# Attention products over all rows and in pairs of heads, and one 512-column product for both operand parts in the 256-token FFNs

## Chip, cores and metric

The kernel runs on one core of a Trainium2 chip. The metric is the device time of one execution in microseconds (us). The engines are named as the profile names them: PE is TensorE's matrix products and PEld its weight loads, DVE is VectorE, ACT is ScalarE, POOL is GpSimd, SP issues the large DMAs.

## What is computed

Two transformer blocks follow each other on 256 tokens of width 1024. The first has two layers with a context of 256 further tokens: a gated linear attention (512 tokens in all) with its FFN, then a latent attention (MLA, 8 heads) whose queries are the 256 main tokens alone, with its FFN. The second block has three mixers side by side, which are 8 heads of dilated attention, a depthwise convolution and 4 heads of attention to a memory of 256 tokens, and then its FFN.

```python
x = x + g1[:, None, :] * o
x = x + g2[:, None, :] * conv_ffn(modulate(x, norm_ffn[i], sh2, sc2), ...)
...
sm = jnp.einsum("bshd,bmhd->bhsm", qm, km).astype(jnp.float32) * (HEAD_DIM ** -0.5)
pm = jax.nn.softmax(sm, axis=-1)
mo = jnp.einsum("bhsm,bmhd->bshd", pm, vm.astype(jnp.float32))
...
f = rms_norm(h, ffn_norm_g[l]) @ w_up[l]
f = depthwise_conv(f, ffn_dw_w[l], ffn_dw_b[l])
fg, fu = jnp.split(f, 2, axis=-1)
h = h + (jax.nn.silu(fg) * fu) @ w_down[l]
```

All is float32. An FFN goes from 1024 to 2 x 2816 features and back, with a convolution over three neighbouring tokens between.

## The kernel before

Activations lie with features on the 128 partitions and tokens along the row: `xT` is 8 tiles of 128 features by 512 tokens, context first (`HALF`, 0 to 255) and main tokens after (`MAIN`, 256 to 511).

**Two parts.** An operand x of a large product is split into hi, x rounded to the matmul's faster float format by ACT, and lo = x - hi on DVE. `mm3` (L320) makes a product of hi.hi, lo.hi and hi.lo, three matmuls (L322 to L324) that add up in one PSUM bank. The weights of one unit come by DMA from SP in tiles of 1 MB (`raw`, three of them), and `ensure_unit` (L279) makes `whi` on ACT (L294) and `wlo` on DVE (L301), four buffers each, three units ahead of the one in use. The activations' parts are `hhi` and `hlo` (`hparts`, L615), in the FFN `ahi` and `alo`.

**FFN.** `ffn` (L1179) runs for i = 0 on 512 tokens, for i = 1 and 2 on 256. Its upward half is 44 units (`proj`, L727): for each, 8 steps of k with one `mm3`, and then an evacuation by `conv3` (L1169), which is one ACT operation (L1172) and two DVE operations (L1175, L1176) on the PSUM bank. Units come in pairs, and after the second of a pair follow SiLU (L1201, ACT), the product (L1202, DVE) and the split into `ahi` and `alo` (L328, L329). The first three units (two for i = 2, `EG`) form a group that goes through k together. The downward half has 8 outputs m, each with 22 steps of k in four weight units (`dn`, L1207), and a residual sum after each: L1125 for i = 1, L1909 for i = 2. For i = 2 the first two units start before the norm is known (`Early`, L699).

**MLA.** `mla_s` (L1506) makes the scores of a head in two tiles of 128 queries by 512 keys: one `mm3`, then two matmuls for the rotary parts. L1512 is over 128 rows (hi and lo of q on the two halves of the rows), L1514 over the 64 rows that hold the hi part. Then follow softmax, transposes (L1542) and the products with V (L1553), each one head behind.

**The second block's mixers.** A pair of heads of 64 features shares one tile of 128 partitions. `qk_post` (L1766) and `m_post` (L1835) scale the queries and write each head into a tile of its own, `qz` or `qmz`, whose other 64 rows are zero. So `at_s` (L1781) multiplies over 128 rows, two float32 products for each head into one bank; float32 products are two instructions each. `at_t` transposes, `at_v` (L1808) multiplies with V into 64 columns of the output. `attention` (L1817) runs head by head, transposes two heads later and P.V three later. Generators (`weave`, `chain`, `braid`) lace these steps with the projections, and taps of the convolution run on DVE, ACT and POOL beside them.

A scheduler orders each engine's queue by readiness and program order; on the chip each engine takes its own queue in order. PSUM has five banks for products (`mmbank`) and three for small things (`smbank`).

## Time and profile before

| | us |
|---|---|
| Median of 3 runs | 1327.21 |
| Lowest and highest | 1323.68, 1330.87 |
| The profiled execution, by its own time | 1330.12 |
| Its span in the trace | 1328.4 |
| Busy: PE / PEld / DVE / ACT / POOL | 1292.8 / 1145.6 / 1053.8 / 722.4 / 85.7 |

The span is the time from the first to the last instruction. Busy is the time in which at least one instruction of the engine runs. Matmuls overlap in their pipeline, so the duration of one is longer than the distance from its start to the next one's. The chain that ended last is followed back from the last instruction, at each step to what released it. The FFN of the first block's second layer runs from about 824 to 1016 us, MLA's heads from about 734 to 774, the second block's mixers from about 1017 to 1115, its FFN from about 1130 to the end.

### The profile page before, as it was taken

To read this page: it belongs to the slowest core of one execution; us is meant where nothing else is said; L and a number is where in the kernel's file an instruction comes from. 1 tells how busy PE (TensorE), PEld (TensorE's weight loads), DVE (VectorE), ACT (ScalarE), POOL (GpSimd) and SP (SyncE) were. 2 spreads that over 40 slices of the span, in tenths; PEclk is the share of its full clock that TensorE was granted. 3 is DMA by queue.
4 is the path that set the end of the run, shared out by engine and by line. 5 is a ranking of instruction groups with operands and counts; after the bars stand their busy time and mean duration, and the time that the engine had idled before them with its cause. 6 is when DMAs were issued, how large, how long until landed. Compare 5 with 4: busy or idle time off the path is not lost.

```text
span 1328.4 us, 21925 instructions
## 1 busy us (share of the span) xinstructions
PE 1292.8 (97%) x8628; PEld 1145.6 (86%) x8628; DVE 1053.8 (79%) x2168; ACT 722.4 (54%) x1241; POOL 85.7 (6%) x101
## 2 busy tenths in 40 slices
PE   6899999999999999999999998999999899999998
PEld 3789888898888888878977698999999788999998
DVE  2598987879999899789667778988657986988853
ACT  4596354444442244433577546766546777766642
POOL 0000000000000000000002054000002610000000
PEclk9999999999999999999999999999999999999999
DMA  9442343325446654436233023555455222455453
GB/s 373 188 146 108 128 169 149 127 96 191 170 149 216 235 193 156 145 131 238 82 112 127 33 78 131 199 179 171 170 200 190 95 96 90 165 191 190 152 190 104
DMA packets 32503, 207.67 MB, mean 156 GB/s; under 512 B 3760, under 2 KB 5040, under 8 KB 12176
## 3 DMA queue, kind: packets, MB, share of 16 engines
q1 hardware_dynamic: 31968, 204.17, 43.3%
q0 software_dynamic: 432, 2.10, 0.5%
q8 instruction: 68, 1.11, 0.3%
q14 instruction: 35, 0.29, 0.1%
HBM read 205.20 MB, written 1.05 MB: 155 GB/s over the span
## 4 chain that ended last, share of the span: by engine, by line
PE 85%; DVE 9%; ACT 2%; DMA 2%; issue 2%; SPq 0%; POOL 0%; DVEq 0%; ACTq 0%; POOLq 0%
PE mm L322 25%; PE mm L324 25%; PE mm L323 25%; DVE wlo L301 2%; DMA raw<-in_w_ada_dram 1%; DVE u L633 1%; PE mm L1553 1%; DVE cacc L1721 1%; PE sm L1003 1%; DMA xT<-in_xT_dram 1%; PE mm L1811 1%; ACT whi L294 1%; PE sm L612 1%; PE sm L797 1%; PE sm L1542 1%
## 5 line engine op out<-in xcount | busy, mean ns | idle before, releaser
L322 PE MATMUL mm<-hhi,whi 128*128 128x256 f32 (+1 forms) x1668 | 534.0, 321 | 1.9 <-ACT hhi L328 0.8
L323 PE MATMUL mm<-hhi,wlo 128*128 128x256 f32 (+1 forms) x1668 | 528.7, 318 | 2.0 <-DVE wlo L301 2.0
L324 PE MATMUL mm<-hlo,whi 128*128 128x256 f32 (+1 forms) x1668 | 525.9, 318 | 1.7 <-DVE hlo L682 1.2
L301 DVE TENSOR_TENSOR wlo<-raw,whi 128x1024 fp32r<-128x1024 f32 (+2 forms) x314 | 350.9, 1119 | 75.4 <-ACT whi L294 73.8
L294 ACT ACTIVATE whi<-raw 128x1024 fp32r<-128x1024 f32 (+2 forms) x316 | 304.5, 969 | 171.1 <-PE mm L324 142.2
L322 PEld LDWEIGHTS mm<-hhi,whi 128*128 128x128 f32 x1668 | 318.4, 191 | 28.9 <-issue 4.6
L323 PEld LDWEIGHTS mm<-hhi,wlo 128*128 128x128 f32 x1668 | 318.8, 191 | 24.1 <-DVE wlo L301 2.4
L324 PEld LDWEIGHTS mm<-hlo,whi 128*128 128x128 f32 x1668 | 317.3, 191 | 24.5 <-DVE hlo L682 2.4
L633 DVE SCALAR_TENSOR_TENSOR u<-raw,cb 128x512 f32<-128x512 f32 x320 | 204.6, 683 | 28.1 <-DMA raw<-in_w_ada_dram 23.1
L324 PE MATMUL mm<-alo,whi 128*128 128x256 f32 (+1 forms) x550 | 171.7, 312 | 0.7 <-DVE alo L329 0.7
L322 PE MATMUL mm<-ahi,whi 128*128 128x256 f32 (+1 forms) x550 | 171.7, 312 | 0.3 <-ACT ahi L328 0.3
L323 PE MATMUL mm<-ahi,wlo 128*128 128x256 f32 (+1 forms) x550 | 171.1, 311 | 0.0
L1172 ACT ACTIVATE cv<-mm,vecs 128x256 f32<-128x256 f32 (+1 forms) x130 | 82.3, 637 | 147.7 <-PE mm L324 144.5
L324 PEld LDWEIGHTS mm<-alo,whi 128*128 128x128 f32 x550 | 104.2, 189 | 7.1 <-DVE alo L329 1.1
L322 PEld LDWEIGHTS mm<-ahi,whi 128*128 128x128 f32 x550 | 104.2, 189 | 6.8 <-ACT ahi L328 0.7
L323 PEld LDWEIGHTS mm<-ahi,wlo 128*128 128x128 f32 x550 | 104.2, 190 | 6.0
L1175 DVE SCALAR_TENSOR_TENSOR cv<-mm,vecs,cv 128x255 f32<-128x255 f32 (+1 forms) x130 | 73.9, 570 | 36.0 <-ACT cv L1172 35.7
L1176 DVE SCALAR_TENSOR_TENSOR cv<-mm,vecs,cv 128x255 f32<-128x255 f32 (+1 forms) x130 | 73.6, 568 | 1.5
L322 PE MATMUL mm<-whi,hhi 128*128 128x256 f32 (+1 forms) x192 | 59.8, 311 | 0.0
L324 PE MATMUL mm<-wlo,hhi 128*128 128x256 f32 (+1 forms) x192 | 58.0, 302 | 0.5 <-DVE wlo L301 0.5
L323 PE MATMUL mm<-whi,hlo 128*128 128x256 f32 (+1 forms) x192 | 57.9, 302 | 0.0
L1201 ACT ACTIVATE cv<-cv 128x256 f32<-128x256 f32 (+1 forms) x66 | 32.2, 488 | 36.9 <-DVE cv L1176 35.6
(318 smaller groups left out, 1390.9 us busy)
## 6 DMA issues: line engine op xcount, KB each, us to landing
raw<-in_up_dram SPq DMA_DIRECT2D x66, 1024.0 KB, 4.9
raw<-in_w_ada_dram SPq DMA_DIRECT2D x40, 1024.0 KB, 4.8
raw<-in_dn_dram SPq DMA_DIRECT2D x48, 704.0 KB, 4.1
raw<-in_gla_in_dram SPq DMA_DIRECT2D x12, 1024.0 KB, 5.4
raw<-in_in_dram SPq DMA_DIRECT2D x9, 1024.0 KB, 4.9
a<-in_ada_dram SPq DMA_DIRECT2D x8, 1024.0 KB, 19.1
raw<-in_gla_out_dram SPq DMA_DIRECT2D x4, 1024.0 KB, 5.5
raw<-in_mla_out_dram SPq DMA_DIRECT2D x4, 1024.0 KB, 4.8
```

The lines of the kernel that those rows point to most:

```text
L294: S.activation(hi[:, :kt * c], r, AF.Copy)
L301: V.tensor_sub(lo[:, :kt * c], r, hi[:, :kt * c])
L322: T.matmul(ps, lhs[0], rhs[0], start=first, stop=False)
L323: T.matmul(ps, lhs[1], rhs[0], start=False, stop=False)
L324: T.matmul(ps, lhs[0], rhs[1], start=False, stop=last)
L612: T.matmul(nb, lhs, self.hl[j], start=(j == 0), stop=(j == 1))
L633: V.scalar_tensor_tensor(tmp(512, "u", 2), raws[n][:, ks], 1.0, cb[:, c, hf * 512:hf * 512 + 512], op0=ALU.mult, op1=ALU.mult, accum_out=p ...
L797: T.matmul(ps[32 * (k % 4):32 * (k % 4) + 32, :256], csil[:, k, :], w_a0[j][:, k, :], start=(k < 4), stop=(k >= 4))
L1172: mark["act"] = S.activation(t[:, :n], ps, AF.Identity, bias=vec(cb, j), scale=vec(cw, 44 + j))
L1175: V.scalar_tensor_tensor(t3[:, :, 1:], p3[:, :, :255], vec(cw, j), t3[:, :, 1:], op0=ALU.mult, op1=ALU.add)
L1176: V.scalar_tensor_tensor(t3[:, :, :255], p3[:, :, 1:], vec(cw, 88 + j), t3[:, :, :255], op0=ALU.mult, op1=ALU.add)
L1201: S.activation(g, g, AF.Silu)
```

## The change

- A weight unit's hi and lo parts lie in one tile `wp`, those of `h` in one tile `hp` and those of the FFN's product in one tile `ap`. A small class `Two` hands out the parts, and `at` gives hi, lo, and both together as one operand of 2 x n columns when n is at most 256.
- In `mm3`, where both together are given and the PSUM slice is 512 wide, one matmul of 512 columns makes hi.hi into the lower half of the bank and hi.lo into the upper, and one of 256 columns adds lo.hi to the upper half. This holds for the FFNs on 256 tokens, but for their first group of units.
- The two halves are added later: in the upward half by an ACT copy of the upper half and a DVE add ahead of `conv3`, which then reads `u` in SBUF; in the downward half by two residual operations instead of one.
- In `mla_s` the last matmul runs over all 128 rows.
- In the second block `qz` and `qmz` go, with their memsets. Queries are scaled in place. `at_s` takes a pair of heads, one on rows 0 to 63, the other on 64 to 127, each into a bank of its own; `at_v` alternates the two heads; `attention` runs by pairs, with transposes and P.V one pair later.

```diff
+            w = wpool.tile([128, 2, 1024], F32R, tag="wp", name="wp", bufs=NUNIT)
+            hi = w[:, 0, :kt * c]
+            S.activation(hi, r, AF.Copy)
...
-                lo = wpool.tile([128, 1024], F32R, tag="wlo", name="wlo", bufs=NUNIT)
-                V.tensor_sub(lo[:, :kt * c], r, hi[:, :kt * c])
+                V.tensor_sub(w[:, 1, :kt * c], r, hi)
+                parts[i, u] = Two(w[:, :, :kt * c].rearrange("p a (k c) -> p k a c", k=kt))
...
+    class Two:
...
+        def at(self, k, s):
+            n = s.stop - s.start
+            return self.t[:, k, 0, s], self.t[:, k, 1, s], self.t[:, k, :, s] if n <= 256 else None
...
     def mm3(ps, lhs, rhs, first, last):
-        T.matmul(ps, lhs[0], rhs[0], start=first, stop=False)
-        T.matmul(ps, lhs[1], rhs[0], start=False, stop=False)
-        T.matmul(ps, lhs[0], rhs[1], start=False, stop=last)
+        if rhs[2] is None or ps.shape[-1] < 512:
+            T.matmul(ps, lhs[0], rhs[0], start=first, stop=False)
+            T.matmul(ps, lhs[1], rhs[0], start=False, stop=False)
+            T.matmul(ps, lhs[0], rhs[1], start=False, stop=last)
+        else:
+            T.matmul(ps.rearrange("p (a t) -> p a t", a=2), lhs[0], rhs[2], start=first, stop=False)
+            T.matmul(ps[:, 256:], lhs[1], rhs[0], start=False, stop=last)
...
+                    if ps.shape[-1] > n:
+                        u = tmp(256, "up", 2)
+                        S.activation(u, ps[:, 256:], AF.Copy)
+                        V.tensor_add(u, ps[:, :256], u)
+                        ps = u
                     hold[half] = conv3(ps, half * FT + j, cw, cb, n, len(halves), f"cv{half}")
...
-            rows = HIGH if hd % 2 else LOW
-            T.matmul(ps, qps[hd][rows, tsl], kps[1][rows], start=False, stop=True)
+            T.matmul(ps, qps[hd][:, tsl], kps[1], start=False, stop=True)
...
-        residual(ps, m, 1, 5, (1,), st[0])
+        residual(ps[:, 256:], m, 1, 5, (1,), None)
+        residual(ps[:, :256], m, 1, 5, (1,), st[0])
...
-            for hf, rows in enumerate((LOW, HIGH)):
-                V.tensor_mul(qz[rows, 2 * m + hf, :], qr[rows, m, :], nb[rows])
+            V.tensor_mul(qr[:, m, :], qr[:, m, :], nb)
...
+    def at_s(p, qt, kt_):
+        pss = [mmbank() for _ in range(2)]
         for t in range(2):
-            T.matmul(ps[:, t * 256:(t + 1) * 256], qt[:, hd, t * 128:(t + 1) * 128], kt_[:, hd // 2, :],
-                     start=True, stop=True)
+            for ps, rows in zip(pss, (LOW, HIGH)):
+                T.matmul(ps[:, t * 256:(t + 1) * 256], qt[rows, p, t * 128:(t + 1) * 128], kt_[rows, p, :],
+                         start=True, stop=True)
+        return pss
...
+    def at_v(p, vsrc, PTs, po):
         for kb in range(2):
-            T.matmul(po[r0:r0 + 64, :256], vsrc[:, kb, hd * 64:(hd + 1) * 64], PT[:, kb * 256:(kb + 1) * 256],
-                     start=(kb == 0), stop=(kb == 1))
+            for hf, PT in enumerate(PTs):
+                c0 = (2 * p + hf) * 64
+                T.matmul(po[64 * hf:64 * hf + 64, :256], vsrc[:, kb, c0:c0 + 64], PT[:, kb * 256:(kb + 1) * 256],
+                         start=(kb == 0), stop=(kb == 1))
...
+    def attention(pairs, qt, kt_, vsrc, m0, masked):
+        Ps, prev = None, None
+        for p in [*pairs, None]:
+            if p is not None:
+                pss = at_s(p, qt, kt_)
                 yield
+            PTs = []
+            for hf in range(2):
+                if p is not None:
+                    new = at_p(pss[hf], masked)
+                    nxt = [new] if hf == 0 else nxt + [new]
+                if Ps is not None:
+                    PTs.append(at_t(Ps[hf]))
                 yield
+            if Ps is not None:
+                po = mmbank()
+                at_v(prev, vsrc, PTs, po)
...
-        V.tensor_add(xT[:, m, MAIN], ps[:, :256], xT[:, m, MAIN])
+        for hs in (MAIN, HALF):
+            V.tensor_add(xT[:, m, MAIN], ps[:, hs], xT[:, m, MAIN])
```

## Rows read from the trace of the kernel before

**Rows 1.** The page, part 1: busy us, share of the span, instructions.

```profile
PE 1292.8 (97%) x8628; PEld 1145.6 (86%) x8628; DVE 1053.8 (79%) x2168; ACT 722.4 (54%) x1241; POOL 85.7 (6%) x101
```

**Rows 2.** The page, part 4: the chain by line, shares of the span.

```profile
PE mm L322 25%; PE mm L324 25%; PE mm L323 25%; DVE wlo L301 2%; DMA raw<-in_w_ada_dram 1%; DVE u L633 1%; PE mm L1553 1%; DVE cacc L1721 1%; PE sm L1003 1%; DMA xT<-in_xT_dram 1%; PE mm L1811 1%; ACT whi L294 1%; PE sm L612 1%; PE sm L797 1%; PE sm L1542 1%
```

**Rows 3.** Stretches: length; busy us (instructions) of PE, PEld, DVE, ACT, POOL; PEclk; DMA.

```profile
740.00:765.00 25.00, 25.00 (x114) 17.81 (x113) 16.69 (x41) 12.04 (x31) 0.00 (x0) 1.00 0.00 1
890.00:920.00 30.00, 30.00 (x252) 30.00 (x252) 25.36 (x43) 19.69 (x33) 0.00 (x0) 1.00 0.52 177
955.00:1015.00 60.00, 60.00 (x517) 59.45 (x516) 37.26 (x60) 30.28 (x47) 3.21 (x3) 1.00 0.59 202
1040.00:1070.00 30.00, 28.54 (x197) 24.94 (x197) 29.60 (x73) 25.65 (x59) 18.34 (x20) 0.97 0.31 106
1070.00:1095.00 25.00, 25.00 (x170) 20.24 (x168) 20.43 (x45) 17.17 (x36) 2.20 (x3) 1.00 0.23 85
1140.00:1170.00 30.00, 29.01 (x237) 28.51 (x237) 29.26 (x52) 22.27 (x40) 2.30 (x3) 1.00 0.47 158
```

**Rows 4.** Timeline, PE, FFN on 256 tokens: start us, duration us, instruction.

```profile
900.02 0.28 PE L324 MATMUL mm<-hlo,whi 128*128 128x256 f32 x1
...
900.38 0.28 PE L324 MATMUL mm<-hlo,whi 128*128 128x256 f32 x1
```

**Rows 5.** Timeline, PE, FFN on 512 tokens.

```profile
400.00 0.39 PE L324 MATMUL mm<-alo,whi 128*128 128x512 f32 x1
...
400.68 0.39 PE L324 MATMUL mm<-alo,whi 128*128 128x512 f32 x1
```

**Rows 6.** Groups by line, form: count; busy us, mean ns; idle before us.

```profile
L800 ACT ACTIVATE u<-sm 128x256 f32<-128x256 f32 x8 | 3.0, 370 | 5.5 <-PE sm L797 5.5
L1889 DVE TENSOR_TENSOR xT<-mm,xT 128x256 f32<-128x256 f32 x8 | 3.3, 417 | 2.1 <-PE mm L324 2.1
```

**Rows 7.** Timeline, DVE, one pair of upward units; idle before in brackets.

```profile
899.50 0.48 DVE L1175 SCALAR_TENSOR_TENSOR cv<-mm,vecs,cv 128x255 f32<-128x255 f32 x1 [0.40 <-ACT cv L1172]
900.02 0.48 DVE L1176 SCALAR_TENSOR_TENSOR cv<-mm,vecs,cv 128x255 f32<-128x255 f32 x1
900.45 1.22 DVE L301 TENSOR_TENSOR wlo<-raw,whi 128x1024 fp32r<-128x1024 f32 x1
901.59 0.42 DVE L1202 TENSOR_TENSOR cv<-cv,cv 128x256 f32<-128x256 f32 x1
902.38 0.48 DVE L1175 SCALAR_TENSOR_TENSOR cv<-mm,vecs,cv 128x255 f32<-128x255 f32 x1 [0.37 <-ACT cv L1172]
902.77 0.42 DVE L329 TENSOR_TENSOR alo<-cv,ahi 128x256 fp32r<-128x256 f32 x1
903.11 0.48 DVE L1176 SCALAR_TENSOR_TENSOR cv<-mm,vecs,cv 128x255 f32<-128x255 f32 x1
```

**Rows 8.** Timeline, ACT, the same pair of units.

```profile
901.78 0.56 ACT L1172 ACTIVATE cv<-mm,vecs 128x256 f32<-128x256 f32 x1 [0.77 <-PE mm L324]
```

**Rows 9.** Timeline, PE, end of one MLA score tile and start of the next.

```profile
746.97 0.39 PE L1512 MATMUL mm<-kp,qps 128*128 128x512 f32 x1
747.29 0.49 PE L1514 MATMUL mm<-kp,qps 64*128 64x512 f32 x1
747.71 0.50 PE L322 MATMUL mm<-kn,hhi 128*128 128x512 f32 x1
748.05 0.40 PE L323 MATMUL mm<-kn,hlo 128*128 128x512 f32 x1
```

**Rows 10.** Timeline, PE, second block's mixers; equal neighbours merged, with their count.

```profile
1084.42 0.64 PE L569 MATMUL sm<-hs,selhalf 128*32 128x256 f32 x8
...
1096.09 3.29 PE L1784 MATMUL mm<-kr,qz 128*128 128x256 f32 x14
...
1101.39 1.08 PE L1811 MATMUL mm<-PT,v 128*64 128x256 f32 x4
...
1106.78 1.68 PE L1811 MATMUL mm<-PT,v 128*64 128x256 f32 x8
```

More of the change, by code (lines that the diff above doesn't have):

```diff
@@ L615, in hparts @@
     def hparts():
-        return (hpool.tile([128, KT, 512], F32R, tag="hhi", name="hhi"),
-                hpool.tile([128, KT, 512], F32R, tag="hlo", name="hlo"))
+        return Two(hpool.tile([128, KT, 2, 512], F32R, tag="hp", name="hp"))
     ada = {l: cpool.tile([128, 2, 48], F32, name=f"ada{l}") for l in range(2)}
@@ L689, in normed_steps @@
         ds = ds or s
[L690 removed]
+        hh, hl = dst[0], dst[1]
         for k in range(KT):
@@ L724, in scaled, with proj @@
             return u
-    def proj(us, h, s, evac, group=3, korder=range(KT), s0=None):
+    def proj(us, h, s, evac, group=3, korder=range(KT), s0=None, apart=False):
         n = s.stop - s.start
+        wide = 512 if apart else n
         s0 = s0 or s
@@ L749, in proj @@
             for a, k in enumerate(ko):
-                mm3(ps[:, :n], (w[0][:, k, :], w[1][:, k, :]), (h[0][:, k, s], h[1][:, k, s]),
+                mm3(ps[:, :wide], (w[0][:, k, :], w[1][:, k, :]), h.at(k, s),
                     a == 0, a == len(ko) - 1)
@@ L753, in proj @@
                     yield
-            evac(ps[:, :n], j)
+            evac(ps[:, :wide], j)
             yield
@@ L767, in gemm_steps @@
         for n, (w, k) in enumerate(kk):
-            mm3(ps, (h[0][:, n, ts], h[1][:, n, ts]), (w[0][:, k, :], w[1][:, k, :]), n == 0, n == len(kk) - 1)
+            mm3(ps, h.at(n, ts), w.at(k, slice(0, 256)), n == 0, n == len(kk) - 1)
             if n == 3:
@@ L843, in first @@
         for t in range(4):
-            mm3(psv[t][:, :256],
-                (h[0][:, k, t * 128:(t + 1) * 128], h[1][:, k, t * 128:(t + 1) * 128]),
-                (w[0][:, kk, :], w[1][:, kk, :]), k == 0, k == KT - 1)
+            mm3(psv[t][:, :256], h.at(k, slice(t * 128, (t + 1) * 128)), w.at(kk, slice(0, 256)),
+                k == 0, k == KT - 1)
     LEAD = 2
@@ L1187, in ffn @@
             phase["pool"] = fp
-            ahi = fp.tile([128, kt, n], F32R, name="ahi")
-            alo = fp.tile([128, kt, n], F32R, name="alo")
+            ap = Two(fp.tile([128, kt, 2, n], F32R, name="ap"))
             hold = {}
@@ L1212, in dn @@
                         mm3(ps, (w[0][:, k - lo_, :], w[1][:, k - lo_, :]),
-                            (ahi[:, k0 + k, ts], alo[:, k0 + k, ts]), first and k == 0, last and k == FG - 1)
+                            ap.at(k0 + k, ts), first and k == 0, last and k == FG - 1)
                     yield
@@ L1232, in ffn @@
             else:
-                f = proj(both([I_up[i, j] for j in range(FT)]), h, s, up_evac(0), s0=early.s0, group=EG) if early else proj(both([I_up[i, j] for j in range(FT)]), h, s, up_evac(0))
+                f = proj(both([I_up[i, j] for j in range(FT)]), h, s, up_evac(0), s0=early.s0, group=EG, apart=True) if early else proj(both([I_up[i, j] for j in range(FT)]), h, s, up_evac(0), apart=True)
                 if early:
@@ L1292, in body @@
     qps = []
-    qns = tuple(x[:, :, MAIN] for x in h)
+    qns = h.sub(slice(0, 8), MAIN)
     pp = ExitStack()
@@ L1335, in body @@
     nb = spread(rr, 512)
-    kvh = tuple(x[:, :4, HALF] for x in h)
+    kvh = h.sub(slice(0, 4), HALF)
     for k in range(2):
@@ L1353, in rope @@
             V.tensor_add(o, a[rows], b[rows])
-    cqh = tuple(x[:, 4:7, HALF] for x in h)
+    cqh = h.sub(slice(4, 7), HALF)
     def kslot(i):
@@ L1673, in body @@
     lcnt = C("lcnt", "cl").rearrange("p (t k) -> p t k", t=2)
-    mix = (h[0][:, :, MAIN], h[1][:, :, MAIN])
+    mix = h.sub(slice(0, 8), MAIN)
     cpad = l2.tile([128, 2, 286], F32, name="cpad")
     G.memset(cpad, 0.0)
-    qz = l2.tile([128, 8, 256], F32, name="qz")
-    G.memset(qz, 0.0)
-    qmz = l2.tile([128, 4, 256], F32, name="qmz")
-    G.memset(qmz, 0.0)
     g8 = l2.tile([128, 2], F32, name="g8")
@@ L1840, in m_post @@
             nb = hds["m"].spread(m)
-            for hf, rows in enumerate((LOW, HIGH)):
-                V.tensor_mul(qmz[rows, 2 * m + hf, :], qm[rows, m, :], nb[rows])
+            V.tensor_mul(qm[:, m, :], qm[:, m, :], nb)
             yield
     drain(proj(both([I_i2[8]]), h, HALF, head_evac("m", [qm[:, m, :] for m in range(2)], [g8[:, 1:2]] * 2), 0))
-    NM = 2
-    g = chain(m_post(), attention(range(NM), qmz, km, vm, 6, False))
+    g = chain(m_post(), attention([0], qm, km, vm, 6, False))
     weave(qk_proj(0), g, 1)
@@ L1851, in body @@
     weave(v_proj2(0), g, 2)
-    g = chain(g, attention(range(4), qz, kr, v2, 0, True))
+    g = chain(g, attention([0, 1], qr, kr, v2, 0, True))
     weave(qk_proj(1), g, 2)
-    g = chain(g, braid(qk_post(1), attention(range(NM, 4), qmz, km, vm, 6, False)))
+    g = chain(g, braid(qk_post(1), attention([1], qm, km, vm, 6, False)))
     weave(v_proj2(1), g, 3)
-    g = chain(g, attention(range(4, 8), qz, kr, v2, 0, True))
+    g = chain(g, attention([2, 3], qr, kr, v2, 0, True))
     def layer_norm():
```

59 lines of the change are left out of this document (22 added, 37 removed).

## The prediction

> **What bounds the kernel now.** I read the page's engine shares first [rows 1], then the chain that ended last [rows 2], then the table of stretches [rows 3]. TensorE (PE) is busy for 97% of the span, and three quarters of the chain lie on the three lines of `mm3`. The table says where this is truly so. In the FFN of the first block's second layer (FFN 1 below; FFN 2 is the second block's) PE is busy all of 30 us of the upward half, and DVE 25.4 of them; in the downward half PE all of 60 us, DVE 37.3. In the first block's attention (MLA) PE is busy 25 of 25 us, DVE 16.7. The second block's attention has two parts: from 1040 to 1070 us DVE is full (29.6 of 30), from 1070 to 1095 PE is (25 of 25). The change touches these places, and each is costed by its own bound.
>
> A busy PE hides gaps, so I price matmuls by the spacing of their starts. At 256 columns three start in 0.36 us, one every 0.120 (900.02 to 900.38) [rows 4]; at 512 columns three start in 0.68, one every 0.227 (400.00 to 400.68) [rows 5]. Two of 256 cost 0.240, one of 512 costs 0.227: so 0.013 us belongs to the instruction and not to its columns.
>
> **FFN matmuls.** Three matmuls of 256 columns (0.360) become one of 512 and one of 256 (0.347): 0.0133 us less for each k. The first three units of FFN 1 and the first two of FFN 2 keep the old path, since their PSUM slice is 256 wide. So FFN 1 upward has (44-3) x 8 = 328, FFN 2 upward (44-2) x 8 = 336, each downward half 8 x 22 = 176. That is 4.4 + 4.5 + 2.3 us for FFN 1 up, FFN 2 up and FFN 2 down. In FFN 1 down the old matmuls already come every 0.116 us (517 in 60 us) [rows 3], so three take 0.348: if the new one of 256 keeps 0.116 the pair takes 0.343 and 0.9 us is won; the bounds are 0.2 (pair at 0.347) and 2.3. I take 0.9. Sum: **-12.1 us**, if nothing else gets late.
>
> The rows show 13 ns per instruction. The Trainium skill ("TensorE: Matmul & The Clock Gate", Back-to-back issue gap) gives the warm gap as N/2.4 + 2.5 ns, which is 109 and 216 ns, and by it the pair would save 2.5 ns. The trace does not agree (120 and 227), and the rows decide; by the page the FFN term would be -2.5 us.
>
> **What the FFN change adds.** Each upward unit but those of the first group gets an ACT copy of the upper half (0.37, as ACT's copy of 256 columns from PSUM) and a DVE add (0.42, as the add of PSUM and SBUF) ahead of `conv3` [rows 6]. ACT, at 19.7 of 30 us [rows 3], takes two copies per pair of units (0.74 in 5.55) and stays below full. DVE is the question. One pair of units takes 16 x 0.36 = 5.76 us, and its eight operations, by spacing, fill: two weight parts 2 x 1.14, two L1175 2 x 0.39, two L1176 2 x 0.43, the product and `alo` 2 x 0.34, which makes 4.60; the rest is waits, 0.40 and 0.37 of them marked, and the spacing of dependent operations [rows 7]. With two adds at 0.34 it fills 5.28, against PE's new 16 x 0.347 = 5.55. So DVE has 0.27 us of waits to spare per pair. Up to there the gain stands; at 0.48 the pair takes 5.76 and the upward gain is nil; beyond, it is a loss. Today's waits are ones for work that does not exist yet: L1175 waits for ACT's L1172, which itself had waited 0.77 us for PE [rows 8]. As DVE falls behind, these go. The new chain is copy, add, L1172, L1175, two changes between ACT and DVE for each unit; a weight part (1.14) fits between the add and L1175, and covers the 0.56 of L1172 [rows 7, 8]. If that cover is missing, each unit waits some 0.6. I take 0.05 us per pair over PE's pace: 41.5 pairs, **+2.0 us** (bounds 0 and the rivals). FFN 2 begins with DVE at 29.3 of 30 us [rows 3], from the normalization: ten units' adds (3.4) meet 0.7 idle there, and up to 2.7 could show on PE, with three units of weights in hand against it; I take **+1.0** (0 to 2.7). The residuals double: L1125 and L1909 run twice per m. Inside the downward half they lie beside PE (DVE 37.3 of 60); the last one of each FFN is on the chain, **+0.9** for both (0.48 as L1176, the same kind and size, and 0.42). FFNs: -12.1 + 2.0 + 1.0 + 0.9 = **-8.2 us**.
>
> **MLA.** The last matmul of each score tile, L1514, is over 64 rows and becomes 128. The starts from L1512 run 746.97, 747.29, 747.71, 748.05: 0.32, 0.42 and 0.34 where 0.227 is the pace: 0.40 us for going to 64 rows and back [rows 9]. The second tile of a head is followed by transposes, which hide some of it (0.35). Seven heads lie where PE is full: 7 x 0.75 = **-5.3 us**; the first one waits for its softmax, 0 to -0.75. What is late next is the softmax, with DVE at 16.7 and ACT at 12.0 of 25 [rows 3]: not full in a period 13% shorter. That L1514's extra rows add a small product of low parts changes nothing in time.
>
> The Trainium skill ("TensorEngine Tiling (Array Packing)", Key Properties) says that a change of tiling mode drains TensorE; the 0.40 agrees. It speaks against the next part, which brings such changes in.
>
> **Second block's attention.** (a) `qz` and `qmz` go: twelve half-height products of 256 columns become six of full height; I price one at the 0.42 of L1202, as many columns [rows 7]. Eight of the twelve lie in the stretch where DVE is full, so 4 x 0.42 = -1.7 us. The two memsets go from POOL, before anything waits for them: nothing. (b) P.V: a head's four matmuls of 64 columns take 1.08 us alone, but eight of two heads took 1.68 (1106.78), though the second head's input came late; eight matmuls of 32 columns took 0.64, where full ones are 0.22 each (3.29 for 14) [rows 10]. So column groups run side by side, and two heads together should cost one. Three pairs in the PE-full part: 3 x 1.08 = -3.2; the last pair overlaps already. (c) Scores: two heads cost 8 x 0.22 = 1.76 today; with both halves of the rows at once, 0.88 plus 0.40 for the mode [rows 9] is 1.28: -0.48 a pair. That row groups overlap no row shows. The nearest is column groups; without overlap a pair costs 1.76 + 0.40, +0.40. Three pairs in or after the PE-full part: -1.4 to +1.2, I take -1.1. (d) A pair's softmax ends later than a head's, and the transposes and P.V wait for both heads; two banks of five go at once: +1.0 (0 to 4). Sum **-5.0 us** (-8 to +3).
>
> The Trainium skill ("TensorE: Matmul & The Clock Gate", Part 3: Packing small matmuls) has row tiles run concurrently as column tiles do; no row here shows it.
>
> **The rest.** Both parts of a weight, or of `h`, now share a tile, with the same readers and writers; a slot came free with the last matmul of its unit before and does so now. Nothing, with up to 1 us either way from reordering.
>
> **Sum.** -8.2 - 5.3 - 5.0 = -18.5 us on the profiled execution's 1330.12 (span 1328.4 and 1.7 around it): 1311.6. The median is 2.9 us lower, 1327.21, and I forecast from it: **1308.7 us**, own range 1302 to 1315.
>
> **Rivals.** (1) DVE sets the pace of the upward halves, evenly: waits of 0.48 a pair, upward gain nil. For it: only 0.27 to spare. Against it: the waits seen are for PE. Left are 3.2 downward less 0.9, MLA and attention: -12.6, 1314.6. (2) Slower: DVE's in-order queue keeps its marked waits of 0.77 and adds the two adds at full 0.42: (5.76 - 0.77) + 0.84 + 0.77 = 6.60 us a pair, 0.84 over today's 5.76, and 41.5 pairs cost 34.9; with the -12.6 this is +22.3, **1349.5**. It decides from 0.48 us of waits a pair on; the total turns slower than before at 0.48 + 12.6/41.5 = 0.78. (3) Row groups do not overlap and pairs lengthen the softmax path: (c) +1.2, (d) +3, attention -0.7: 1313. (4) The new path saves less than it says: the instruction's share is what FFN 1's downward rows make it, 2 x 0.116 - 0.227 = 0.005, and 1016 pairs save 5.1 instead of 12.1: 1315.7. For it: those rows; against it: they are one stretch of four. By the page named above it would be still less. (5) (1) and (3) together: -8.3, 1319, and some more waits put it within 0.5% of before.
>
> **Chances.** Forecast 0.50, (1) 0.14, (2) 0.10, (3) 0.13, (4) 0.05, (5) 0.08. About 0.5% is what a measurement of this kernel can tell from none: faster is below 1320.6, slower above 1333.8. The forecast, (1), (3), (4) and half of (5) are faster, less 0.04 for unlucky sums: 0.82; same 0.08; slower 0.10. The range takes in (1), (3), (4), (5) and a little below the forecast's own: 1300 to 1324.
>
> **What would show it.** Right: in the upward halves starts alternate 0.227 and 0.120, PE stays full and DVE is near 95%; L1514 spaced 0.227; in a pair's scores starts of both row halves within some ns; the same in P.V. Wrong: PE in FFN 1 or 2 waiting for `wp` from DVE, or for PSUM; starts of a pair's row halves 0.22 apart; PE idle behind the softmax at the end of the second attention.

## The result

| | us | against before |
|---|---|---|
| Changed kernel, median of 5 runs | 1312.12 (1309.43 to 1316.80) | 0.9895 (0.9865 to 0.9926) |
| The same kernel once more, median of 4 runs | 1311.87 (1309.19 to 1313.24) | 0.9877 (0.9857 to 0.9897) |
| Profiled execution, and its span | 1309.43, 1307.7 | |

A ratio is given with its 95% interval, against runs of the kernel before on the same chip. The change makes the kernel faster by 1.05% to 1.23%, which is 13.9 to 16.3 us of before's median. The forecast was 1308.7 us with a range of 1300 to 1324; the median lies 3.4 us above it.

The profile after, first its busy time (share of the span, instructions) and the chain by engine and by line, which answer to [rows 1] and [rows 2]:

```profile
PE 1265.2 (97%) x7612; PEld 1082.2 (83%) x7612; DVE 1076.0 (82%) x2261; ACT 748.3 (57%) x1324; POOL 84.8 (6%) x99
...
PE 82%; DVE 9%; ACT 4%; DMA 2%; issue 2%; POOL 1%; SPq 0%; POOLq 0%; DVEq 0%; ACTq 0%
PE mm L345 18%; PE mm L341 16%; PE mm L343 15%; PE mm L342 15%; PE mm L346 9%; DVE wp L301 2%; DMA a<-in_ada_dram 1%; DVE u L654 1%; ACT wp L295 1%; PE mm L1577 1%; DMA raw<-in_w_ada_dram 1%; PE sm L1024 1%; PE mm L1837 1%; PE sm L634 1%; PE mm L1046 1%
```

PE is as full as before, with 27.6 us less to do. The new lines L345 (512 columns) and L346 (256) carry 27% of the chain. The stretches of the profile after, in the order of [rows 3] (length; busy us and instructions of PE, PEld, DVE, ACT, POOL; granted clock; DMA):

```profile
736.00:762.00 26.00, 26.00 (x141) 22.48 (x140) 19.13 (x45) 14.27 (x36) 0.00 (x0) 1.00 0.00 1
876.00:906.00 30.00, 30.00 (x175) 26.43 (x175) 29.81 (x56) 23.97 (x45) 0.00 (x0) 1.00 0.53 194
942.00:1002.00 60.00, 60.00 (x388) 54.01 (x388) 40.33 (x67) 31.73 (x48) 0.57 (x1) 1.00 0.57 199
1028.00:1058.00 30.00, 27.33 (x199) 23.09 (x198) 29.57 (x70) 25.97 (x60) 19.32 (x21) 0.96 0.31 106
1058.00:1083.00 25.00, 25.00 (x188) 20.04 (x187) 20.58 (x48) 17.63 (x38) 2.20 (x3) 1.00 0.25 88
1126.00:1156.00 30.00, 29.00 (x164) 24.85 (x165) 29.08 (x55) 24.09 (x45) 1.67 (x3) 1.00 0.40 140
```

In the upward half of FFN 1 (second row) PE does 175 matmuls where it did 252 [rows 3], as two replace three. DVE went from 25.36 to 29.81 of 30 us there, and PE still has no gap.

Because the stages follow each other, the time of each can be read between fixed points of the traces. I use four: MLA from the first matmul of its rotary scores to its last product with V; FFN 1 from the copy of the memory's keys ahead of it to the first copy of the gated unit behind it; the second attention from there to the first residual of its output projection; FFN 2 from the last of these residuals to the end.

| us in the trace | MLA | FFN 1 | second attention | FFN 2 |
|---|---|---|---|---|
| before | 47.59 | 209.63 | 100.89 | 195.61 |
| after | 43.41 | 204.66 | 97.92 | 189.80 |
| after, the second execution | 43.38 | 204.58 | 98.16 | 193.05 |
| forecast difference | -5.3 | -3.8 | -5.0 | -4.4 |
| difference of the first two | -4.2 | -5.0 | -3.0 | -5.8 |

The forecast's four sums are those of its text, with the waits of the upward halves shared evenly between the FFNs. The measured differences add to -18.0, and the spans differ by 20.7. The 2.7 us between are 4.0 less in the first 55 us of the program, where nothing was changed, and 1.3 more elsewhere outside the four stages: the first matmul of the first projection starts at 54.69 in before and at 50.65 in after, and over all the profiles of this study that point lies between 49.3 and 54.7, also for one with before's code there (49.28). The profile of before was simply a long one (1330.12, where the median of 29 later runs is 1326.22).

### The profile page after: what moved, and what is told of

Same layout as the page of the kernel before. It is cut to its first block, busy times and chain, and to the rows that moved or that the text cites. A ratio compares the mean times of both kernels' runs of the same rounds, so it can differ in the third digit from the quotient of the medians.

```text
span 1307.7 us, 20138 instructions
## 1 busy us (share of the span) xinstructions
PE 1265.2 (97%) x7612; PEld 1082.2 (83%) x7612; DVE 1076.0 (82%) x2261; ACT 748.3 (57%) x1324; POOL 84.8 (6%) x99
## 3 DMA queue, kind: packets, MB, share of 16 engines
HBM read 205.20 MB, written 1.05 MB: 158 GB/s over the span
## 4 chain that ended last, share of the span: by engine, by line
PE 82%; DVE 9%; ACT 4%; DMA 2%; issue 2%; POOL 1%; SPq 0%; POOLq 0%; DVEq 0%; ACTq 0%
PE mm L345 18%; PE mm L341 16%; PE mm L343 15%; PE mm L342 15%; PE mm L346 9%; DVE wp L301 2%; DMA a<-in_ada_dram 1%; DVE u L654 1%; ACT wp L295 1%; PE mm L1577 1%; DMA raw<-in_w_ada_dram 1%; PE sm L1024 1%; PE mm L1837 1%; PE sm L634 1%; PE mm L1046 1%
## 5 line engine op out<-in xcount | busy, mean ns | idle before, releaser
L301 DVE TENSOR_TENSOR wp<-raw,wp 128x1024 fp32r<-128x1024 f32 (+2 forms) x314 | 350.5, 1118 | 63.8 <-ACT wp L295 63.0
L295 ACT ACTIVATE wp<-raw 128x1024 fp32r<-128x1024 f32 (+2 forms) x316 | 305.0, 970 | 168.5 <-PE mm L343 87.8
L341 PE MATMUL mm<-hp,wp 128*128 128x512 f32 (+1 forms) x1004 | 346.4, 346 | 2.3 <-ACT hp L350 1.7
L342 PE MATMUL mm<-hp,wp 128*128 128x512 f32 (+1 forms) x1004 | 342.5, 342 | 3.1 <-DVE wp L301 3.1
L343 PE MATMUL mm<-hp,wp 128*128 128x512 f32 (+1 forms) x1004 | 338.8, 341 | 0.9 <-DVE hp L703 0.9
L345 PE MATMUL mm<-hp,wp 128*128 128x512 f32 x664 | 231.3, 394 | 0.6 <-DVE hp L351 0.5
L341 PEld LDWEIGHTS mm<-hp,wp 128*128 128x128 f32 x1004 | 191.6, 191 | 30.2 <-issue 5.7
L342 PEld LDWEIGHTS mm<-hp,wp 128*128 128x128 f32 x1004 | 192.1, 191 | 24.7 <-DVE wp L301 3.5
L343 PEld LDWEIGHTS mm<-hp,wp 128*128 128x128 f32 x1004 | 190.8, 191 | 22.7 <-DVE hp L703 1.6
L346 PE MATMUL mm<-hp,wp 128*128 128x256 f32 x664 | 184.4, 278 | 0.6 <-DVE wp L301 0.6
L345 PEld LDWEIGHTS mm<-hp,wp 128*128 128x128 f32 x664 | 124.4, 187 | 29.8 <-DVE hp L351 0.9
L346 PEld LDWEIGHTS mm<-hp,wp 128*128 128x128 f32 x664 | 125.0, 188 | 1.5 <-DVE wp L301 0.9
L345 PE MATMUL mm<-ap,wp 128*128 128x512 f32 x352 | 122.1, 392 | 0.0
L346 PE MATMUL mm<-ap,wp 128*128 128x256 f32 x352 | 98.4, 279 | 0.0
L1193 ACT ACTIVATE cv<-mm,vecs 128x512 f32<-128x512 f32 (+1 forms) x47 | 35.5, 765 | 78.5 <-PE mm L343 75.4
L345 PEld LDWEIGHTS mm<-ap,wp 128*128 128x128 f32 x352 | 66.0, 188 | 14.6
L343 PE MATMUL mm<-ap,wp 128*128 128x512 f32 (+1 forms) x198 | 72.5, 366 | 0.7 <-DVE ap L351 0.7
L341 PE MATMUL mm<-ap,wp 128*128 128x512 f32 (+1 forms) x198 | 72.7, 367 | 0.4 <-ACT ap L350 0.4
L342 PE MATMUL mm<-ap,wp 128*128 128x512 f32 (+1 forms) x198 | 72.4, 366 | 0.0
L346 PEld LDWEIGHTS mm<-ap,wp 128*128 128x128 f32 x352 | 66.3, 188 | 0.0
```

The lines of the kernel that those rows point to most:

```text
L295: S.activation(hi, r, AF.Copy)
L301: V.tensor_sub(w[:, 1, :kt * c], r, hi)
L341: T.matmul(ps, lhs[0], rhs[0], start=first, stop=False)
L342: T.matmul(ps, lhs[1], rhs[0], start=False, stop=False)
L343: T.matmul(ps, lhs[0], rhs[1], start=False, stop=last)
L345: T.matmul(ps.rearrange("p (a t) -> p a t", a=2), lhs[0], rhs[2], start=first, stop=False)
```

## Experiments

Ratios are against before, as above. All edits marked "before with" start from the kernel before, the others from the changed one.

### One part at a time

**The layout alone.** Weights, `h` and the FFN's inner operand in shared tiles, every product still three of 256 columns; MLA, the second attention and the residual sums as before (that part of the edit is not shown).

```diff
-        return self.t[:, k, 0, s], self.t[:, k, 1, s], self.t[:, k, :, s] if n <= 256 else None
+        return self.t[:, k, 0, s], self.t[:, k, 1, s], None
...
-        wide = 512 if apart else n
+        wide = n
```

> Only the layout of the change: both parts of a weight, of h and of the FFN's inner operand share a tile, but every product is still three of 256 columns; no copy, no add, residuals as before, MLA and second attention as before. Forecast: 0, within 1 us either way. Rival L (the layout itself makes the start 4 us shorter, as the two profiles have it, or moves the order of the work): -2 to -5 us, with the first 50 us of the trace shorter.

Measured: 1327.06 us, ratio 1.0007 (0.9991 to 1.0022). The layout costs and brings nothing that can be told, and the short start is not its doing: the time of the start differs between executions of equal code.

**MLA alone**, before with

```diff
-            rows = HIGH if hd % 2 else LOW
-            T.matmul(ps, qps[hd][rows, tsl], kps[1][rows], start=False, stop=True)
+            T.matmul(ps, qps[hd][:, tsl], kps[1], start=False, stop=True)
```

> The kernel before with one edit: in the first block's attention (MLA) the last matmul of a score tile runs over all 128 rows, not over the 64 of its head. Theory M (a matmul over 64 rows costs a round trip of 0.40 us between row modes; the part of it that transposes hide stays hidden): 7 to 8 heads at 0.5 to 0.75 us, so -3.5 to -6 us against before, all of it between the first score and the last P.V of MLA, and the starts from the second-last score matmul to the next at 0.227 us. Rival (the round trip is not on the path, since the softmax comes late behind it): 0, within 1.5 us. After's trace has -4.2 us in this stage; if the stage alone gives clearly less here, a part of those 4.2 came from the change's other edits.

Measured: 1322.39 us, ratio 0.9975 (0.9961 to 0.9989), which is -3.3 us (-5.2 to -1.5); the stage takes 42.75 us, 4.84 less. Theory M stands. The timeline of PE shows why (start us, duration us, instruction); L1513 is the matmul that was over 64 rows:

```profile
743.74 0.40 PE L1512 MATMUL mm<-kp,qps 128*128 128x512 f32 x1
743.97 0.39 PE L1513 MATMUL mm<-kp,qps 128*128 128x512 f32 x1
744.20 0.39 PE L322 MATMUL mm<-kn,hhi 128*128 128x512 f32 x1
```

Every start is 0.23 us behind the last; in [rows 9] the same steps took 0.32, 0.42 and 0.34.

**The pairs alone**, before with the changed `qk_post`, `m_post`, `at_s` to `attention`, and without `qz` and `qmz`.

> The kernel before with the second block's attention alone as after has it: scores and P.V in pairs of heads, q scaled in place without the zero-padded copies; FFNs and MLA as before. Theory A (column and row groups overlap, a pair's P.V is cut in two when its first PT comes early): -2 to -4 us, of which the DVE-full part from 1040 us on gives none itself. Rival B (the pairs only pay because FFN and glu before them end earlier relative to DVE's queue): 0 to -1. Rival C (as forecast, -5). The score starts of a pair's two row halves should lie some ns apart in any of them.

Measured: 1325.68 us, ratio 0.9994 (0.9979 to 1.0009): no difference that can be told. The stage takes 99.91 us, 1.0 less than before, where it is 3.0 less in after with the same code. The two agree in the part where PE is full (from the last pair's first evacuation to the first residual): 51.6 us in before, 48.6 in both. They differ in the part ahead of it: 42.6 us in before and in after, 44.6 here. The stretches of this kernel show where (columns as above):

```profile
1023.40:1043.40 20.00, 16.11 (x119) 14.68 (x117) 19.28 (x29) 15.32 (x33) 13.77 (x14) 0.91 0.44 159
...
1047.40:1051.40 4.00, 1.85 (x17) 1.47 (x19) 4.00 (x11) 2.29 (x8) 0.85 (x1) 0.99 0.00 0
1051.40:1068.00 16.60, 16.60 (x115) 13.49 (x108) 14.61 (x35) 13.21 (x27) 9.79 (x11) 0.90 0.38 127
```

and the same places in after:

```profile
1011.10:1031.10 20.00, 16.11 (x114) 14.54 (x114) 19.10 (x29) 15.20 (x32) 13.72 (x14) 0.83 0.44 158
...
1035.10:1039.10 4.00, 2.98 (x27) 2.19 (x26) 4.00 (x12) 3.42 (x9) 1.86 (x1) 1.00 0.02 4
1039.10:1053.70 14.60, 14.60 (x107) 12.23 (x108) 14.56 (x33) 12.73 (x26) 9.75 (x11) 1.00 0.42 144
```

PE pauses here for a softmax, 2.15 us in the pairs alone and 1.02 in after. Behind the longer pause the granted clock of the next 16.6 us is 0.90, that is a part of them at the lower level (1.2 of 2.4 GHz); behind the shorter one it stays at 1.00. The first rows belong to the account: ahead of the pause it is after that has the lower clock, 0.83 over 20 us against 0.91. So in the pairs alone PE comes to the pause 0.7 us earlier and waits longer; the softmax itself ends 0.5 us later (both counted from the first evacuation), and with some 1.7 us of lost clock behind it (16.6 x 0.10) that is about the 2 us that separate the two. Over the whole part both lose the same clock (20 x 0.17 is 3.4 us; 20 x 0.09 and 16.6 x 0.10 are 3.5), but in after all of it falls ahead of the pause, which takes a part of it up. By its number the run is rival B's, but B's reason does not hold: the kernel with the product cut back (below) has the other edits, and takes 44.5 us for this part and 99.84 for the stage. The pairs' code took 97.9 to 100.0 us in six profiles, before's code 100.9 to 101.8 in four, so the gain is 0.9 to 3.9 us from one execution to the next.

**The FFNs alone**: the change without the MLA edit and without the pairs.

> The change without its MLA edit and without the paired attention: merged weight and operand tiles, the 512-column product in both 256-token FFNs with its copy and add upward, and the doubled residual additions. Theory F (13.3 ns for each of 1016 pairs, less the additions at either end of an FFN): -8 to -11 us, -3.8 to -5.3 in FFN 1 and -4.4 to -5.8 in FFN 2 between their first and last convolution plus the downward half. Rival G (the instruction's own share is 5 ns, the rest of after's gain is order): -2 to -5. In the trace the starts of an upward half alternate 0.230 and 0.117 us under F; under G they sum to 0.352 or more.

Measured: 1316.33 us, ratio 0.9928 (0.9906 to 0.9951), -9.5 us (-12.5 to -6.5). FFN 1 takes 204.58 us (-5.0), FFN 2 189.85 (-5.8). Theory F stands; G would have had less than half.

The three parts (the layout is in the last) make -3.3, -0.8 and -9.5, so -13.6 in sum, against -13.9 and -16.3 measured for all together.

### The price of an instruction

The product of 512 columns cut back into two of 256, in the same halves of the bank:

```diff
-            T.matmul(ps.rearrange("p (a t) -> p a t", a=2), lhs[0], rhs[2], start=first, stop=False)
+            T.matmul(ps[:, :256], lhs[0], rhs[0], start=first, stop=False)
+            T.matmul(ps[:, 256:], lhs[0], rhs[1], start=False, stop=False)
             T.matmul(ps[:, 256:], lhs[1], rhs[0], start=False, stop=last)
```

> The changed kernel with the product of 512 columns cut back into two of 256, in the same two halves of the bank: the copies, the adds and the doubled residual sums stay, only the number of matmuls goes back from two to three for each of 1016 k. Theory N (the share of an instruction is 0.0133 us, which the FFN's gain rests on): the steps of k come every 0.360 us, 0.3533 in FFN 1's downward half, as before the change; FFN 1 and FFN 2 lose 12.4 us together against after, to about 1324.5. Rival (the gain comes from the other edits in the FFN, such as the shared tiles or the later use of the sum): under 4 us lost. A third way: the steps come at 0.3533 in one FFN or both, as they did in FFN 2 of one execution of the changed kernel with two matmuls; then half of the 12.4 is lost there.

Measured: 1321.76 us, ratio 0.9953 (0.9934 to 0.9973), some 8 to 10 us above after (by the ratios, 0.58% to 0.76%). FFN 1 takes 210.38 us, 5.7 more than after, FFN 2 195.95, 6.15 more: 11.9 of the 12.4 forecast. Theory N stands. Upward halves of after and then of this kernel, on PE:

```profile
899.86 0.39 PE L345 MATMUL mm<-hp,wp 128*128 128x512 f32 x1
900.09 0.28 PE L346 MATMUL mm<-hp,wp 128*128 128x256 f32 x1
900.21 0.39 PE L345 MATMUL mm<-hp,wp 128*128 128x512 f32 x1
900.44 0.28 PE L346 MATMUL mm<-hp,wp 128*128 128x256 f32 x1
900.55 0.39 PE L345 MATMUL mm<-hp,wp 128*128 128x512 f32 x1
```

```profile
890.00 0.28 PE L345 MATMUL mm<-hp,wp 128*128 128x256 f32 x1
890.12 0.28 PE L346 MATMUL mm<-hp,wp 128*128 128x256 f32 x1
890.24 0.28 PE L347 MATMUL mm<-hp,wp 128*128 128x256 f32 x1
890.36 0.28 PE L345 MATMUL mm<-hp,wp 128*128 128x256 f32 x1
```

A step of k takes 0.345 us in the first (899.86 to 900.21 and 900.55) and 0.36 in the second. All else in the FFN is the same, so the gain belongs to the third instruction.

### What the additions on ACT and DVE cost

Without the copy and the add in the upward halves; the convolution then reads the lower half of the bank only.

```diff
-                        u = tmp(256, "up", 2)
-                        S.activation(u, ps[:, 256:], AF.Copy)
-                        V.tensor_add(u, ps[:, :256], u)
-                        ps = u
+                        ps = ps[:, :n]
```

> The changed kernel without the ACT copy and the DVE add in the upward halves of the two FFNs on 256 tokens: the convolution reads the lower half of the bank alone, so the sum of the two halves is left out. Theory H (the additions lie beside PE, whose pace is the bound; after's upward halves won 4.1 and 3.9 us of 4.4 and 4.5 to be had): -0.3 to -1.5 us against after. Rival (DVE at 95% costs PE 0.05 us a pair of units and 1 us at either FFN's beginning, as forecast): -3 to -4.

Measured: 1313.51 us, ratio 0.9896 (0.9878 to 0.9915), 1.6 us above the changed kernel's second median, 1311.87; no gain. FFN 1 takes 204.60 us (after: 204.66 and 204.58), FFN 2 193.04 (after's second execution: 193.05, at the same pace of PE; on the two paces see the last section). In the FFNs the additions cost nothing that can be seen, less than even theory H allowed. The small difference of the whole is not in the FFNs: MLA took 45.08 us in this profile, at a mean clock of 0.96.

With a second DVE operation of the same size for each unit, which nobody reads:

```diff
                         V.tensor_add(u, ps[:, :256], u)
+                        V.tensor_add(tmp(256, "upd", 2), u, u)
```

> The changed kernel with a second DVE operation of the add's size (0.34 us by spacing) in each upward unit of the two FFNs, into a tile that nobody reads. Nothing else changes. Theory D (the forecast's point of decision: DVE has 0.27 us a pair of units to spare before it sets the pace): the pair takes 0.68 more of DVE, 0.41 more than there is, for 41.5 pairs, +17 us (13 to 20) against after. Rival W (DVE's busy time still holds waits that it can give up): under +5 us.

Measured: 1332.39 us, ratio 1.0037 (1.0021 to 1.0052), 20.5 us above the changed kernel's 1311.87. FFN 1 takes 215.67 us (+11.0) and FFN 2 200.70 (+10.9). A stretch of FFN 1's upward half, of after and then of this kernel:

```profile
880.00:910.00 30.00, 30.00 (x175) 26.47 (x174) 29.79 (x58) 23.90 (x45) 0.00 (x0) 1.00 0.54 201
```

```profile
880.00:910.00 30.00, 27.10 (x151) 22.81 (x150) 28.24 (x58) 22.00 (x40) 0.00 (x0) 1.00 0.50 176
```

DVE does 58 operations in 30 us either way, and PE falls from 175 matmuls to 151. Theory D stands: the loss is 21.9 us over 41.5 pairs of units, 0.53 a pair, for 0.68 us of added work, so 0.15 us were free where the forecast had 0.27. DVE itself is not quite full in this stretch, 28.24 of 30: it waits 1.8 us for ACT's step of the convolution (L1193), so that the pace is set by the chain of the two. And 3.4 of the 21.9 us lie in the downward halves (62.73 and 62.49 us where after has 60.90), where PE still waits for weight parts from DVE (1.2 us in FFN 1's). The change lies just on the good side of an edge: one DVE operation more for each unit would have turned it into a small loss.

### P.V and the order of two heads

In after a pair's P.V is often cut in two. PE's timeline (x: how many instructions):

```profile
1079.59 0.65 PE L1837 MATMUL mm<-PT,vm 128*64 128x256 f32 x2
1080.16 1.13 PE L1806 MATMUL mm<-kr,qr 64*128 64x256 f32 x6
1081.22 1.08 PE L1837 MATMUL mm<-PT,vm 128*64 128x256 f32 x6
1082.23 1.56 PE L1806 MATMUL mm<-kr,qr 64*128 64x256 f32 x10
```

Two of the eight run as soon as the first head's PT is there, six after other work: 0.57 and 1.01 us to the next start. Taking the later head first should keep the eight together.

```diff
-            for hf, PT in enumerate(PTs):
+            for hf, PT in reversed(list(enumerate(PTs))):
```

> The changed kernel, with the two heads of a pair in P.V in the other order, the later one first. The first matmul then waits for the later PT, so that the scheduler has no head to start alone, and the eight matmuls should stay together (1.01 us where a split pair takes 0.58 + 1.01). Theory S (the split is what P.V lost against the forecast): three pairs in the part where PE is full, -1.2 to -1.8 us against after. Rival (PE waits for the later PT instead): 0 or slower, with idle time of PE ahead of P.V.

Measured: 1317.05 us, ratio 0.9919 (0.9903 to 0.9935), 5.2 us slower than the changed kernel's 1311.87. The eight do stay together, and P.V itself gets cheaper, as theory S has it: 5.96 us from start to next start in the part where PE is full, instead of 7.50. But the stage takes 104.74 us instead of 98: the rival holds too and outweighs it, with an addition. Timeline of PE, then the clock of the stretches around it:

```profile
1085.76 1.08 PE L1837 MATMUL mm<-PT,vm 128*64 128x256 f32 x8 [1.48 <-ACT PT L1830]
1086.78 2.00 PE L1806 MATMUL mm<-kr,qr 64*128 64x256 f32 x16
1090.23 0.72 PE L1827 MATMUL sm<-ca,P 128*128 128x128 f32 x4 [1.46 <-DVE P L1526]
...
1094.96 1.98 PE L1837 MATMUL mm<-PT,v 128*64 128x256 f32 x8
```

```profile
1085.00:1090.00 5.00, 3.01 (x24) 1.95 (x24) 3.69 (x13) 2.68 (x10) 0.00 (x0) 1.00 0.48 159
1090.00:1098.00 8.00, 7.07 (x41) 4.32 (x42) 4.39 (x21) 4.71 (x15) 0.00 (x0) 0.58 0.08 32
```

PE now waits 1.48 us for the later PT and 1.46 for the softmax behind it, and after these pauses the granted clock is 0.58 for 8 us, most of it at the lower level: the next P.V takes 1.98 us instead of 1.08. In the part where PE is full its idle time grows from 3.2 to 6.2 us. So the split halves had been filling pauses, as far as these rows show.

### The stretch in which DVE is full

Two kernels ask for the taps of the convolution later: one tap for each call of `take()`, and three for each step of the last attention; in the second, one tap in the first eight calls only.

```diff
-    def take(n=2):
-        TP, TK = 1, 2
+    def take(TK=1):
+        TP = 1
...
-        take()
+        take(3)
```

> The changed kernel with one tap of the convolution on DVE for each call of take() instead of two, and three for each step of the last attention: DVE taps move out of the stretch in which DVE is full and POOL busy (a tap is marked 0.95 us there beside POOL's additions, 0.47 otherwise) into the stretch after it. Theory V (DVE's time sets the end of that stretch, as the forecast took it): 8 taps of 0.4 to 0.9 us go, the stretch from the memory head's evacuation to the last pair's first (42.6 us in after) gets 3 to 6 us shorter, and the whole 1 to 4 us, since the taps come back later where DVE has 4.4 us free of 25. Rival Q (PE's queue and the softmax set it, DVE is only full because taps fill its waits): the stretch stays within 1 us of 42.6, and the whole is 0 to +4 us.

> As the run before it, but only the first eight calls of take() are down to one tap; all later ones take three. Fewer taps are left for the end, where the layer norm waits for them. Theory V: the stretch shorter by 2 to 5 us and the whole by 1 to 4. Rival Q: 42.6 within 1 us, the whole 0 to +2.

Measured: 1313.31 us, ratio 0.9899 (0.9880 to 0.9918), and 1313.75, 0.9889 (0.9872 to 0.9907). The stretch takes 42.54 and 43.0 us (after: 42.56 and 42.84). That looks like rival Q, but the edit did not do what it was meant to: DVE ran 26 taps in this stretch in both, as many as in after. The scheduler, which orders by readiness, put them back. So these two runs decide nothing.

The zero-padded queries back, with pairs, lag and P.V as in the change:

```diff
-            V.tensor_mul(qr[:, m, :], qr[:, m, :], nb)
+            for hf, rows in enumerate((LOW, HIGH)):
+                V.tensor_mul(qz[rows, 2 * m + hf, :], qr[rows, m, :], nb[rows])
...
-            for ps, rows in zip(pss, (LOW, HIGH)):
-                T.matmul(ps[:, t * 256:(t + 1) * 256], qt[rows, p, t * 128:(t + 1) * 128], kt_[rows, p, :],
+            for hf, ps in enumerate(pss):
+                T.matmul(ps[:, t * 256:(t + 1) * 256], qt[:, 2 * p + hf, t * 128:(t + 1) * 128], kt_[:, p, :],
```

> The changed kernel with the zero-padded query tiles and their twelve half-height products back, so that the scores of a pair run over 128 rows one head after the other; pairs, lag and P.V stay as in the change. Theory K (as forecast: 1.7 us of DVE in the full stretch and 0.48 us of PE for each pair): +2 to +3 us against after. Theory Q (DVE's full stretch does not follow DVE's work): only the scores' part, +0.5 to +1.5 us, all of it after the end of the full stretch.

Measured: 1313.11 us, ratio 0.9903 (0.9879 to 0.9927), against 0.9877 for the changed kernel: 1 to 3 us slower, which the intervals can't tell from none. The stage takes 101.11 us, 3.2 more than after. Theory K's sum (2 to 3) is near that, but the scheduler changed the order too: the evacuation that ends the full stretch comes 4.5 us earlier (38.0 us), with 22 taps ahead of it instead of 26, and the rest is 7.7 us longer (56.4). The parts of K and Q can't be told apart by it.

**The changed kernel again.**

> The changed kernel itself once more, beside the next three. The single edits gave -3.3 us (MLA), -0.8 (pairs), -9.5 (FFNs) and +0.9 (layout alone) against before, so if they add up it lies 13 to 14 us under before, near 1312.5. If the stages of its profile (-18.3 in sum) were right as they stand, it would be near 1308. The first 50 us of its profile should differ from the first profile's by some us, since nothing there was changed and equal code gave 49.3 to 54.7 so far.

Measured as in the first table. Its stages add to -14.5 against before, the first profile's to -18.0; the whole difference is FFN 2, 193.05 against 189.80.

## Why the prediction was right, and where it was not

**The direction and the size** were right: forecast -18.5, measured -13.9 and -16.3, and -14.5 to -18.0 by the stages of two profiles. That the sum is so near is in part luck: in the first profile the FFNs gave 2.6 us more than forecast and the two attentions 3.1 less, which cancelled. In the second the FFNs gave 7.6, 0.6 less than forecast, since PE ran FFN 2 at another pace (last section), which was not foreseen.

**FFN matmuls: right.** 13.3 ns for each pair in three of the four halves: a step of k comes every 0.345 to 0.347 us, and it comes at 0.36 again when the instruction is put back. FFN 1's downward half, priced between 0.2 and 2.3 with 0.9 taken, gave 1.2 (62.07 to 60.90 us from its first matmul to its last), which is 6.7 ns a pair; FFN 2's gave 2.3 (63.24 to 60.90), as forecast. Where FFN 2 runs at the slower pace, it gains 6.7 ns a pair too. Rival (4) is out: putting the instruction back cost 11.9 us.

**What the FFN change adds: too dear.** The step that failed is "I take 0.05 us per pair over PE's pace", +2.0 us, and the +1.0 taken for FFN 2's beginning. Both are nothing: without the additions neither FFN is any faster. The waits that stood between DVE's operations [rows 7] went, as the text argued, and all of them, not all but 0.05. The last residual sums were put at +0.9; FFN 2's gave +0.47 (the time from the last product to the end, 3.64 in before, 4.11 in after) and FFN 1's none (15.28 and 15.27 us from the last product to the next stage). So the FFNs gave -10.8 where -8.2 stood. By these terms alone it would be -11.9 (-12.1, 0.3 more in FFN 1's downward half, +0.47 at the end); the missing 1.1 us is not accounted for, and it is missing without the additions as well. Rivals (1) and (2) did not come, but the mechanism that they name is real: 0.68 us more of DVE a pair cost 20.5 us. The timeline of DVE in after shows how near it is:

```profile
899.63 1.21 DVE L301 TENSOR_TENSOR wp<-raw,wp 128x1024 fp32r<-128x1024 f32 x1
900.77 0.42 DVE L1227 TENSOR_TENSOR cv<-cv,cv 128x256 f32<-128x256 f32 x1
901.10 0.48 DVE L1196 SCALAR_TENSOR_TENSOR cv<-up,vecs,cv 128x255 f32<-128x255 f32 x1
901.50 0.41 DVE L1221 TENSOR_TENSOR up<-mm,up 128x256 f32<-128x256 f32 x1
901.83 0.47 DVE L1197 SCALAR_TENSOR_TENSOR cv<-up,vecs,cv 128x255 f32<-128x255 f32 x1
902.22 1.22 DVE L301 TENSOR_TENSOR wp<-raw,wp 128x1024 fp32r<-128x1024 f32 x1
```

Each operation starts before the last one's end, without one marked wait, where [rows 7] had 0.40 and 0.37. The order changed too: the add of one unit (L1221) runs between the two convolution steps of the unit before, so that a copy on ACT and the change of engine lie behind other work, not on DVE's path.

**MLA: the mechanism right, the sum 1.1 us too large.** The 64-row mode cost what [rows 9] said, and it is gone. What comes late next was named (the softmax) and put at nothing. PE's waits in this stage, in before and then in after (us in total, times, longest):

```profile
PE mm L1553 <- ACT PT L1545: 0.4, 1, 0.4
```

```profile
PE mm L1577 <- ACT PT L1569: 1.3, 1, 1.3
PE sm L1566 <- DVE xT L1526: 0.5, 1, 0.5
PE mm L341 <- ACT xT L1523: 0.4, 1, 0.4
```

That is 2.2 us in three waits for the softmax and the PT made from it, where one wait of 0.4 was: 1.8 us more, which is more than the difference between -5.3 and -4.2.

**Second attention: the step that failed is (a), and (b) and (d) were each off by about 1 us.** In the part where PE is full the sum came out by luck: -3.0 measured, -3.3 forecast without (a). But 0.9 of the 3.0 are four score instructions of 28 that after runs ahead of this part, and the terms themselves make -2.1. (b) gave -2.2 and not -3.2: PE's P.V there takes 7.50 us, start to next start, instead of 9.67, because most pairs are cut in two. (c) is right: row groups do run side by side,

```profile
1072.21 1.13 PE L1806 MATMUL mm<-km,qm 64*128 64x256 f32 x8
1073.27 0.38 PE L341 MATMUL mm<-wp,hp 128*128 128x256 f32 x1
```

eight instructions of two heads in 1.06 us to the next start, those of the two row halves 6 ns apart, where eight over all rows take 1.80 by the spacing of their starts [rows 10]; over the three pairs, with the changes of mode inside them, it is 3.68 us, 1.23 a pair, which makes -1.7 for (c) where -1.1 was taken. Rival (3), which needs the row groups not to overlap, is out. The Trainium skill ("TensorE: Matmul & The Clock Gate", Part 3: Packing small matmuls) says that tiles on different rows run concurrently, and the trace agrees (1.06 against 1.80 us). (d) is +1.8 us of PE's idle time (1.37 to 3.17), with +1.0 taken from 0 to 4.

(a) gave nothing. The four multiplications of queries that went were 1.7 us of DVE in a stretch where DVE is full, and the stretch is as long as before: 42.56 and 42.58 us. DVE did other work in their place, 26 taps instead of 22. And a tap's price depends on POOL (DVE, then POOL, in after):

```profile
1036.18 0.46 DVE L1742 SCALAR_TENSOR_TENSOR cacc<-cpad,vecs,cacc 128x256 f32<-128x256 f32 x1
...
1048.45 0.94 DVE L1742 SCALAR_TENSOR_TENSOR cacc<-cpad,vecs,cacc 128x256 f32<-128x256 f32 x1
...
1050.19 0.96 DVE L1742 SCALAR_TENSOR_TENSOR cacc<-cpad,vecs,cacc 128x256 f32<-128x256 f32 x1
```

```profile
1033.80 0.92 POOL L1376 TENSOR_TENSOR rb<-kr,cos 128x256 f32<-128x256 f32 x1
1037.04 1.86 POOL L1376 TENSOR_TENSOR rb<-kr,cos 128x256 f32<-128x256 f32 x1 [2.32 <-ACT kr L1760]
...
1046.71 7.52 POOL L1732 TENSOR_TENSOR cacp<-cacp,cvp 128x256 f32<-128x256 f32 x8
```

0.46 us while POOL idles, 0.94 and 0.96 while it adds; the 15 taps of after that meet no POOL instruction take 0.38 to 0.49. So to take DVE's work as the price because [rows 3] show DVE full was the wrong reading: a part of what fills DVE there is work that could run later (the four taps more), and a part is an operation made longer by POOL. The Trainium skill ("SBUF — State Buffer", Who interferes with whom) says that a DVE instruction with two SBUF inputs, as a tap is, contends with a GpSimd instruction that reads SBUF; the doubled taps agree with it. Whether DVE or the softmax behind it sets the length of this stretch stays open: the two runs meant to tell kept the same order.

## What to carry to other kernels

Where PE is full, count matmul instructions and not only columns: here each cost 0.013 us beyond its columns (0.007 in the halves that ran at another pace), and a second PSUM half with an add elsewhere buys one in three back, as long as the engine that adds keeps below its edge, which is worth probing with one dummy operation. Waits of an off-path engine for the bound engine are spare time that can be spent: here two additions for each pair of units fitted in, and 0.15 us was left. A stretch in which an engine is full through work that could run later need not be bound by that engine, and taking work from it may give nothing; and a pause of PE costs more than its length when the granted clock falls behind it, as in two of the runs here.
